# Routing of a mixture-of-experts block: the tokens' low parts formed by VectorE from PSUM instead of by GpSimd, and two selection chains interleaved

## The chip, the cores and the metric

The kernel is one program on one core of a Trainium2 chip. The core has a matrix engine (TensorE, PE in the rows; its weight loads are PEld), VectorE (DVE), ScalarE (ACT), GpSimd (POOL) and a queue that issues transfers (SP). Matrix products land in PSUM, which has eight banks per partition; all else is in SBUF. Each engine works through its own list of instructions in the order in which it was written or scheduled, and engines wait for each other by semaphores. The metric is device microseconds of one execution; the time of a kernel is the median of its runs.

## The reference, cut to what matters

Two layers over 256 tokens of width 1024. Each layer adds a mix of a convolution and two attentions, then a mixture of 16 experts in four groups. The change is in the routing of the experts:

```python
def grouped_moe(h, w_router, b_router, w_gate, w_up, w_down):
    aff = sigmoid(h @ w_router)
    biased = aff + b_router
    grp = biased.reshape(B, L, 4, 4)
    grp_score = sum(top_k(grp, 2)[0], axis=-1)          # sum of the two best of a group
    best = argmax(grp_score)                             # one group for each token
    in_grp = (arange(16) // 4) == best[..., None]
    _, top_idx = top_k(where(in_grp, biased, -inf), 2)   # its two best experts
    w = take(aff, top_idx); w = w / sum(w)
    ...
    for e in range(16):
        a = silu(h @ w_gate[e]) * (h @ w_up[e])
        out = out + gates[..., e:e+1] * (a @ w_down[e])
```

So a token picks the group whose two best scores have the largest sum, and in it the two experts with the best scores; ties go to the lower index.

## The kernel before, in words

**Weights.** All weights come from HBM through one ring of 14 buffers of 1 MB (`pump`, L77), issued on SP's queue in a fixed order: of a layer first the projections of the mixers and the modulation (ada) parts, then eight pairs of experts, for each pair four tiles of gate and up weights and two of down weights. A buffer that TensorE has finished (`done`) is issued again for the next tile in the list.

**A layer.** The mixers end with the output projection (L645) and the residual (L396), which also feeds the router's logits (L388, L392). Then `moe` begins with `route`. The token tile is transposed back to token-major order into four PSUM banks (`xtp[h, t]`, L901 and L903: half h of the columns, tokens t). In layer 1 these four banks are not given back, as the experts' results are later added onto them (`accs`). In `route`, VectorE works out scores, groups and experts; TensorE meanwhile runs matmuls for the next modulation vectors (`fill(2)`, L274).

**The tokens in two parts.** The gather needs the normalised tokens as a sum of a rounded value `gH` and its remainder `gL`. Before, ScalarE scales each bank into a tile `xs` (L798) and rounds it into `gH` (L799), and GpSimd forms `gL = xs - gH` (L800), four pieces of 128x512 in each layer.

**Selection.** It is two chains on VectorE. The first finds the group (L755 to L772: `hi`, `lo`, `m1` to `m3`, `gs`, `gm`, `ing`), on 2 to 16 elements a partition. The second counts for each expert how many of its group beat it (L779 to L784: `eql`, `gtr`, `ct`), on 128 elements. `slb` (L787) joins them to a 0/1 table in bf16.

**Counts, one-hots, gather.** TensorE turns `slb` into positions within each expert's block (L803 to L807). VectorE makes keys from them (L811 to L828), then `prep1(0)` writes the one-hot table `D` of the first four experts' pairs (L910). `prep4` gathers the tokens (L935): for each of eight column blocks four matmuls, `gH` and `gL` of token tile 0, then of tile 1, added up in PSUM; two column blocks share a bank. ScalarE evicts the first and third bank (L939), VectorE the second and fourth (L941). Then the experts of pair 0 start (L957), with the weights' buffers that wait for that.

**Layer 1 alone.** The vector g2 is spread over all partitions by two matmul groups (L883) into two banks, which VectorE adds to a table (L1110) right after `D`.

TensorE's and VectorE's orders in `moe` are as the code writes them (`manual_schedule`); ScalarE and GpSimd are ordered by the tile scheduler.

Of the kernel before, what the change touches and what calls it, by code (L numbers as in the profile page):

```python
# [9 lines left out]
F32 = mybir.dt.float32  # L10
# [3 lines left out]
AF = mybir.ActivationFunctionType  # L14
OP = mybir.AluOpType
# [4 lines left out]
P = 128  # L20
# [32 lines left out]
def block_kernel(ctx: ExitStack, tc: tile.TileContext, x, c, w_ada, b_ada, g_mix, w_in, w_dw, b_dw, ln_conv_g,  # L53
# [673 lines left out]
    def route(wk, router, xtp, gH, gL, fill):  # L727
# [16 lines left out]
        for t in range(NT):  # L744
# [7 lines left out]
        b8 = bi.rearrange("p t (g e) -> p (t g) e", e=4)  # L752
        hi = tmp([P, 8, 2], "hi")
        lo = tmp([P, 8, 2], "lo")
        V.tensor_tensor(hi, b8[:, :, 0:4:2], b8[:, :, 1:4:2], OP.max)  # L755
        V.tensor_tensor(lo, b8[:, :, 0:4:2], b8[:, :, 1:4:2], OP.min)
        m1 = tmp([P, 8], "m1")
# [4 lines left out]
        V.tensor_tensor(m3, lo[:, :, 0], lo[:, :, 1], OP.max)  # L762
        V.tensor_tensor(m2, m2, m3, OP.max)
        gs = tmp([P, NT, 4], "gs")
        V.tensor_tensor(gs.rearrange("p t g -> p (t g)"), m1, m2, OP.add)
        gm = tmp([P, NT, 1], "gm")
        V.tensor_reduce(gm[:, :, 0], gs, AX.X, OP.max)
        V.tensor_tensor(gs, gs, gm.to_broadcast([P, NT, 4]), OP.is_equal)
# [4 lines left out]

        shp = [P, 8, 4, 4]
        mine = b8[:, :, :, None].to_broadcast(shp)
        other = b8[:, :, None, :].to_broadcast(shp)
        gtr, eql = (wk.tile([P, FE], F32, name=n, tag="eac")[:, 0:8 * 16].rearrange("p (g a b) -> p g a b", g=8, a=4)
                    for n in ("gtr", "eql"))
        V.tensor_tensor(eql, other, mine, OP.is_equal)  # L779
        V.tensor_tensor(gtr, other, mine, OP.is_gt)  # L780
        V.tensor_tensor(eql, eql, low4[:, None, :, :].to_broadcast(shp), OP.mult)
        V.tensor_tensor(gtr, gtr, eql, OP.add)
        ct = wk.tile([P, FE], F32, name="ct", tag="eth", bufs=1)[:, 0:32].rearrange("p (g e) -> p g e", e=4)
        V.tensor_reduce(ct, gtr, AX.X, OP.add)  # L784
# [7 lines left out]
        for h in range(2):  # L792
            for t in range(NT):
                hs = slice(h * 512, (h + 1) * 512)
                if t == 0:
                    xs2 = wk.tile([P, NT, 512], F32, name="xs", tag="Yh")
                xs = xs2[:, t, :]
                S.activation(xs, xtp[h, t], AF.Copy, scale=rst[:, t:t + 1])  # L798
                S.copy(gH[:, t, hs], xs)  # L799
                G.tensor_tensor(gL[:, t, hs], xs, gH[:, t, hs].bitcast(F32), OP.subtract)  # L800
# [508 lines left out]
```

## Time and profile before

| | before |
|---|---|
| median of 3 runs | 592.02 us (590.42 to 594.18) |
| profiled execution | 592.18 us, span 590.5 us from first to last instruction |
| TensorE busy | 548.6 us, 93% of the span |
| VectorE busy | 277.8 us, 47% |
| ScalarE busy | 157.6 us, 27% |
| GpSimd busy | 46.0 us, 8% |
| HBM read | 180.92 MB, 308 GB/s over the span |
| mean granted clock of TensorE | 0.976 of full |

The routing of layer 0 stands at about 162 to 181 us of the span, that of layer 1 at about 442 to 460 us. The profile cannot be read from the busy shares alone: an engine with a small share can hold up the one that is nearly always busy, and it does so only in the stretches where that one stands idle. So the rows to look for are idle times of TensorE and what ended them.

### The profile page before, as it was taken

To read this page: it belongs to the slowest core of one execution; us is meant where nothing else is said; L and a number is where in the kernel's file an instruction comes from. 1 tells how busy PE (TensorE), PEld (TensorE's weight loads), DVE (VectorE), ACT (ScalarE), POOL (GpSimd) and SP (SyncE) were. 2 spreads that over 40 slices of the span, in tenths; PEclk is the share of its full clock that TensorE was granted. 3 is DMA by queue.
4 is the path that set the end of the run, shared out by engine and by line. 5 is a ranking of instruction groups with operands and counts; after the bars stand their busy time and mean duration, and the time that the engine had idled before them with its cause. 6 is when DMAs were issued, how large, how long until landed. Compare 5 with 4: busy or idle time off the path is not lost. (4 is left out here: it accounts for less than half of the span.)

```text
span 590.5 us, 10358 instructions
## 1 busy us (share of the span) xinstructions
PE 548.6 (93%) x3881; PEld 336.7 (57%) x3881; DVE 277.8 (47%) x882; ACT 157.6 (27%) x368; POOL 46.0 (8%) x51
## 2 busy tenths in 40 slices
PE   2889999999979999999969999999997999999993
PEld 0378886677735444444337788668774554444331
DVE  1321999574264433332133099956427533333222
ACT  1331103346242111111134021344624211111114
POOL 1000004000030000000000000500003011111110
PEclk9979999999989999999979999999998999999997
DMA  8999989973499999999999997957349699999932
GB/s 320 383 302 380 401 316 394 398 268 116 140 335 363 363 363 354 359 348 359 391 352 372 384 383 308 347 196 246 122 143 332 199 360 361 359 363 361 356 112 75
DMA packets 126025, 182.82 MB, mean 310 GB/s; under 512 B 7920, under 2 KB 94216, under 8 KB 125960
## 3 DMA queue, kind: packets, MB, share of 16 engines
q1 hardware_dynamic: 125344, 180.80, 88.2%
q10 hardware_dynamic: 616, 1.19, 0.5%
q8 instruction: 36, 0.59, 0.4%
q14 instruction: 29, 0.24, 0.1%
HBM read 180.92 MB, written 1.05 MB: 308 GB/s over the span
## 5 line engine op out<-in xcount | busy, mean ns | idle before, releaser
L957 PE MATMUL bank<-w,XT 128*32 128x512 f32 (+1 forms) x1024 | 112.9, 592 | 0.0
L431 PE MATMUL bank<-w,hT 128*128 128x256 f32 (+1 forms) x448 | 102.9, 390 | 1.1 <-ACT hT L407 1.1
L431 PEld LDWEIGHTS bank<-w,hT 128*128 128x128 f32 x448 | 85.6, 193 | 16.9 <-ACT hT L407 2.1
L957 PEld LDWEIGHTS bank<-w,XT 128*32 128x32 f32 x1024 | 33.6, 110 | 75.1 <-issue 69.3
L995 PE MATMUL bank<-w,eaT 128*32 128x512 f32 (+1 forms) x512 | 58.2, 595 | 0.4
L645 PE MATMUL bank<-yT,w 128*128 128x256 f32 x256 | 57.5, 381 | 0.0
L274 PE MATMUL bank<-w,cB 128*32 128x512 f32 x384 | 50.8, 641 | 5.7 <-DMA w<-in_w_ada 3.5
L645 PEld LDWEIGHTS bank<-yT,w 128*128 128x128 f32 x256 | 48.0, 190 | 6.8 <-issue 0.7
L674 DVE SCALAR_TENSOR_TENSOR cvy<-cva,hw,cvy 128x256 f32<-128x256 f32 x108 | 49.7, 509 | 0.6
L945 DVE SCALAR_TENSOR_TENSOR eac<-eth,bank 128x256 f32<-128x256 f32 x16 | 6.7, 421 | 83.5 <-ACT eth L944 83.5
L935 PE MATMUL bank<-D,gH 128*128 128x256 f32 x128 | 33.1, 297 | 2.4 <-DVE eac L945 2.4
L995 PEld LDWEIGHTS bank<-w,eaT 128*32 128x32 f32 x512 | 15.2, 110 | 32.0 <-issue 28.9
L944 ACT ACTIVATE eth<-bank 128x256 f32<-128x256 f32 x16 | 6.1, 384 | 96.2 <-PE bank L957 96.2
L935 PE MATMUL bank<-D,gL 128*128 128x256 f32 x128 | 31.2, 282 | 0.0
L939 ACT ACTIVATE XT<-bank,sh,sc 128x256 f32<-128x256 f32 x36 | 18.2, 560 | 44.4 <-PE bank L935 44.4
L935 PEld LDWEIGHTS bank<-D,gH 128*128 128x128 f32 x128 | 24.7, 193 | 6.7 <-issue 4.7
L446 PE MATMUL bank<-hT,w 128*128 128x256 f32 x128 | 28.3, 379 | 0.0
L446 PEld LDWEIGHTS bank<-hT,w 128*128 128x128 f32 x128 | 24.2, 190 | 3.3
L274 PEld LDWEIGHTS bank<-w,cB 128*32 128x32 f32 x384 | 10.6, 112 | 26.7 <-issue 16.5
L983 POOL TENSOR_TENSOR Yl<-yf,Yh 128x512 fp32r<-128x512 f32 x14 | 18.0, 1283 | 95.1 <-ACT Yh L982 95.1
L522 ACT ACTIVATE pr<-pr,nm 128x128 f32<-128x128 f32 (+1 forms) x48 | 21.3, 444 | 14.1 <-DVE nm L519 14.1
L935 PEld LDWEIGHTS bank<-D,gL 128*128 128x128 f32 x128 | 24.7, 193 | 0.2 <-issue 0.2
(268 smaller groups left out, 662.9 us busy)
## 6 DMA issues: line engine op xcount, KB each, us to landing
w<-in_w_ada SPq DMA_DIRECT2D x48, 1024.0 KB, 11.6
w<-in_w_gate SPq DMA_DIRECT2D x128, 256.0 KB, 6.1
w<-in_w_up SPq DMA_DIRECT2D x128, 256.0 KB, 5.9
w<-in_w_down SPq DMA_DIRECT2D x64, 512.0 KB, 7.5
w<-in_w_in SPq DMA_DIRECT2D x16, 1024.0 KB, 13.0
w<-in_w_o SPq DMA_DIRECT2D x8, 1024.0 KB, 9.1
w<-in_w_in SPq DMA_DIRECT2D x4, 328.0 KB, 15.8
xin<-in_x ACTq DMA_DIRECT2D x1, 1024.0 KB, 9.4
```

The costliest lines, as they stand in the source:

```text
L274: T.matmul(self.pa[j:j + 32, :], cB[:, 2 * kq + kk, o:o + 32], W[:, kk, h * 512:(h + 1) * 512], start=(u == 0 and kq == 0), stop=(u + 1 == ...
L431: T.matmul(pts[t], hT[:, k, tt], W[:, kk, :], start=first, stop=last)
L446: T.matmul(pp[:, cc, :], W[:, kk, cs], hT[:, k, :], start=(k == 0 and cc == 0), stop=(k == KT - 1 and cc == 1))
L522: S.activation(pr[:, lo:hi], pr[:, lo:hi], AF.Exp, bias=nm[:, u:u + 1], scale=-1.0, accum_out=sums[:, u:u + 1])
L645: T.matmul(pos[n // 2][:, n % 2, :], W[:, n * P:(n + 1) * P], yT[:, k, :], start=(ki == 0 and n % 2 == 0), stop=(ki == KT - 1 and n % 2 == 1))
L674: tap = V.scalar_tensor_tensor(out=cy[:, cc, :], in0=src, scalar=w, in1=cy[:, cc, :], op0=OP.mult, op1=OP.add)
L935: T.matmul(pg[:, i, :], z[:, t, ks], D[:, t, :], start=(si == 0), stop=(si == 3))
L939: S.activation(XT[:, k, :], pg[:, i, :], AF.Identity, bias=sh2[:, k:k + 1], scale=a2[:, k:k + 1])
L945: V.scalar_tensor_tensor(out=ac, in0=th, scalar=1.0, in1=pgu[:, 0, :], op0=OP.add, op1=OP.mult)
L957: T.matmul(pf[b0:b0 + BLK, :], XT[:, k, o + b0:o + b0 + BLK], W[:, e, k % 2, :], start=(k == 0), stop=(k == KT - 1))
L983: (V if whole else G).tensor_tensor(Yl[:, sl], yf, Yh[:, sl].bitcast(F32), OP.subtract)
L995: T.matmul(pd[b0:b0 + BLK, :], aT[:, f, b0:b0 + BLK], W[:, e, f, :], start=(f == 0), stop=(f == 1))
```

## The change

In `route`, the `xs` tile, the second ScalarE pass and GpSimd's subtraction are gone. ScalarE scales and rounds each PSUM bank straight into `gH` (four instructions a layer instead of eight). A generator `low()` forms `gL = bank * rst - gH` on VectorE, reading the PSUM bank; `moe` runs it right after `prep1(0)`, so behind `D` and ahead of the g2 additions and the gather's evictions. The selection's two chains are written alternately. Nothing else is touched.

```diff
--- before.py
+++ after.py
@@ -750,38 +750,38 @@
         V.scalar_tensor_tensor(out=bi, in0=aff, scalar=0.5, in1=brt[:, None, :].to_broadcast([P, NT, NE]), op0=OP.mult,
                                op1=OP.add)
         b8 = bi.rearrange("p t (g e) -> p (t g) e", e=4)
+
+        shp = [P, 8, 4, 4]
+        mine = b8[:, :, :, None].to_broadcast(shp)
+        other = b8[:, :, None, :].to_broadcast(shp)
+        gtr, eql = (wk.tile([P, FE], F32, name=n, tag="eac")[:, 0:8 * 16].rearrange("p (g a b) -> p g a b", g=8, a=4)
+                    for n in ("gtr", "eql"))
+        ct = wk.tile([P, FE], F32, name="ct", tag="eth", bufs=1)[:, 0:32].rearrange("p (g e) -> p g e", e=4)
         hi = tmp([P, 8, 2], "hi")
         lo = tmp([P, 8, 2], "lo")
         V.tensor_tensor(hi, b8[:, :, 0:4:2], b8[:, :, 1:4:2], OP.max)
         V.tensor_tensor(lo, b8[:, :, 0:4:2], b8[:, :, 1:4:2], OP.min)
+        V.tensor_tensor(eql, other, mine, OP.is_equal)
         m1 = tmp([P, 8], "m1")
         m2 = tmp([P, 8], "m2")
         m3 = tmp([P, 8], "m3")
         V.tensor_tensor(m1, hi[:, :, 0], hi[:, :, 1], OP.max)
         V.tensor_tensor(m2, hi[:, :, 0], hi[:, :, 1], OP.min)
         V.tensor_tensor(m3, lo[:, :, 0], lo[:, :, 1], OP.max)
+        V.tensor_tensor(gtr, other, mine, OP.is_gt)
         V.tensor_tensor(m2, m2, m3, OP.max)
+        V.tensor_tensor(eql, eql, low4[:, None, :, :].to_broadcast(shp), OP.mult)
         gs = tmp([P, NT, 4], "gs")
         V.tensor_tensor(gs.rearrange("p t g -> p (t g)"), m1, m2, OP.add)
+        V.tensor_tensor(gtr, gtr, eql, OP.add)
         gm = tmp([P, NT, 1], "gm")
         V.tensor_reduce(gm[:, :, 0], gs, AX.X, OP.max)
+        V.tensor_reduce(ct, gtr, AX.X, OP.add)
         V.tensor_tensor(gs, gs, gm.to_broadcast([P, NT, 4]), OP.is_equal)
         V.tensor_tensor(gs, gs, desc4[:, None, :].to_broadcast([P, NT, 4]), OP.mult)
         V.tensor_reduce(gm[:, :, 0], gs, AX.X, OP.max)
         ing = tmp([P, NT, 4], "ing")
         V.tensor_tensor(ing, gs, gm.to_broadcast([P, NT, 4]), OP.is_equal)
-
-        shp = [P, 8, 4, 4]
-        mine = b8[:, :, :, None].to_broadcast(shp)
-        other = b8[:, :, None, :].to_broadcast(shp)
-        gtr, eql = (wk.tile([P, FE], F32, name=n, tag="eac")[:, 0:8 * 16].rearrange("p (g a b) -> p g a b", g=8, a=4)
-                    for n in ("gtr", "eql"))
-        V.tensor_tensor(eql, other, mine, OP.is_equal)
-        V.tensor_tensor(gtr, other, mine, OP.is_gt)
-        V.tensor_tensor(eql, eql, low4[:, None, :, :].to_broadcast(shp), OP.mult)
-        V.tensor_tensor(gtr, gtr, eql, OP.add)
-        ct = wk.tile([P, FE], F32, name="ct", tag="eth", bufs=1)[:, 0:32].rearrange("p (g e) -> p g e", e=4)
-        V.tensor_reduce(ct, gtr, AX.X, OP.add)
         ingb = ing.rearrange("p t g -> p (t g)")[:, :, None].to_broadcast([P, 8, 4])
         slb = wk.tile([P, NT, NE], BF16, name="slb", tag="slb", bufs=1)
         V.scalar_tensor_tensor(out=slb.rearrange("p t (g e) -> p (t g) e", e=4), in0=ct, scalar=1.5, in1=ingb,
@@ -791,13 +791,7 @@
         fill(2)
         for h in range(2):
             for t in range(NT):
-                hs = slice(h * 512, (h + 1) * 512)
-                if t == 0:
-                    xs2 = wk.tile([P, NT, 512], F32, name="xs", tag="Yh")
-                xs = xs2[:, t, :]
-                S.activation(xs, xtp[h, t], AF.Copy, scale=rst[:, t:t + 1])
-                S.copy(gH[:, t, hs], xs)
-                G.tensor_tensor(gL[:, t, hs], xs, gH[:, t, hs].bitcast(F32), OP.subtract)
+                S.activation(gH[:, t, h * 512:(h + 1) * 512], xtp[h, t], AF.Copy, scale=rst[:, t:t + 1])
         slf = sl.rearrange("p (t g) e -> p t (g e)", t=NT)
         pk = bank([P, NT + 1, NE])
         T.matmul(pk[:, 0, :], tri, slb[:, 0, :], start=True, stop=True)
@@ -827,6 +821,14 @@
         V.tensor_copy(ky[:, :, :, 1:3], rk2)
         V.tensor_scalar(ky[:, :, :, 3], rk2[:, :, :, 1], float(-BLK), None, OP.add)
 
+        def low():
+            for h in range(2):
+                for t in range(NT):
+                    hs = slice(h * 512, (h + 1) * 512)
+                    V.scalar_tensor_tensor(out=gL[:, t, hs], in0=xtp[h, t], scalar=rst[:, t:t + 1],
+                                           in1=gH[:, t, hs].bitcast(F32), op0=OP.mult, op1=OP.subtract)
+                    yield
+
         def gates():
             S.activation(lg, lg, AF.Exp, scale=-1.0)
             V.tensor_scalar(lg, lg, 1.0, None, OP.add)
@@ -863,7 +865,7 @@
             V.tensor_scalar(fl[:, 0:1], m1x, CAP + 0.5, None, OP.is_gt)
             return fl, nb
 
-        return ky, gates, flags, rk, fi
+        return ky, gates, flags, rk, fi, low()
 
     def moe(big, wk, l, router, nxt, nnorm):
         a2, sh2 = mod["sc2", l], mod["sh2", l]
@@ -903,7 +905,7 @@
                         T.transpose(pt[:, j * P:(j + 1) * P], xk, ident)
                 xtp[h, t] = pt
 
-        ky, gates, flags_, rk, fi = route(wk, router, xtp, gH, gL, fill)
+        ky, gates, flags_, rk, fi, low = route(wk, router, xtp, gH, gL, fill)
         kyf = ky.rearrange("p t q b -> p t (q b)")
 
         def onehot(key, D, nb, w):
@@ -1106,6 +1108,8 @@
             gather(d["XT"], d["D"], 2 * P, kps, act)
 
         prep1(0)
+        for _ in low:
+            pass
         for h, pb in enumerate(g2ps):
             V.tensor_tensor(g2b[:, h * 512:(h + 1) * 512], pb, g2b[:, h * 512:(h + 1) * 512], OP.add)
         prep4(0, range(4))
```

How the order moves at three places. The first is VectorE in layer 0, within the selection; `bi` are the biased scores, `hi`, `lo`, `m`, `gs`, `gm`, `ing` belong to the group's chain, `eql`, `gtr`, `ct` to the count's. Before:

```order
L765 TENSOR_TENSOR gs<-m_1356,m_1357 128x8 [waits DVE_49]
L767 TENSOR_REDUCE gm<-gs 128x2 [waits DVE_49]
L768 TENSOR_TENSOR gs<-gs,gm 128x8 [waits DVE_49]
L769 TENSOR_TENSOR gs<-gs,desc_81 128x8 [waits DVE_49]
L770 TENSOR_REDUCE gm<-gs 128x2 [waits DVE_49]
L772 TENSOR_TENSOR ing<-gs,gm 128x8 [waits DVE_49]
L779 TENSOR_TENSOR eql<-bi 128x128
L780 TENSOR_TENSOR gtr<-bi 128x128
L781 TENSOR_TENSOR eql<-eql,low_82 128x128 [waits DVE_49]
L782 TENSOR_TENSOR gtr<-gtr,eql 128x128 [waits DVE_49]
L784 TENSOR_REDUCE ct<-gtr 128x32 [waits DVE_49]
L787 SCALAR_TENSOR_TENSOR slb<-ct,ing 128x32 [waits DVE_49]
```

and with the change:

```order
L764 TENSOR_TENSOR eql<-bi 128x128
L768 TENSOR_TENSOR m_1360<-hi 128x8 [waits DVE_49]
L769 TENSOR_TENSOR m_1361<-hi 128x8
L770 TENSOR_TENSOR m_1362<-lo 128x8 [waits DVE_49]
L771 TENSOR_TENSOR gtr<-bi 128x128
L772 TENSOR_TENSOR m_1361<-m_1361,m_1362 128x8 [waits DVE_49]
L773 TENSOR_TENSOR eql<-eql,low_82 128x128
L775 TENSOR_TENSOR gs<-m_1360,m_1361 128x8 [waits DVE_49]
L776 TENSOR_TENSOR gtr<-gtr,eql 128x128 [waits DVE_49]
L778 TENSOR_REDUCE gm<-gs 128x2 [waits DVE_49]
L779 TENSOR_REDUCE ct<-gtr 128x32 [waits DVE_49]
L780 TENSOR_TENSOR gs<-gs,gm 128x8 [waits DVE_49]
```

The five wide instructions stood in a row behind `ing`; now each stands between two small ones of the other chain.

The second is VectorE in layer 1, behind the keys `ky`; `bank_7844` and the three like it hold the transposed tokens, `rst` the tokens' scales. Before:

```order
L828 TENSOR_SCALAR ky<-rk 128x16
L910 TENSOR_TENSOR D<-iota_s,ky 128x512 [waits DVE_49]
L1110 TENSOR_TENSOR g2b<-bank_7969,g2b 128x512 [waits DMAHW3_49,PE_49]
L1110 TENSOR_TENSOR g2b<-bank_7971,g2b 128x512 [waits PE_49]
L941 TENSOR_SCALAR XT<-bank_8000,sc_1_7478,sh_1_7476 128x256 [waits PE_49]
```

and with the change:

```order
L912 TENSOR_TENSOR D<-iota_s,ky 128x512 [waits DVE_49]
L828 SCALAR_TENSOR_TENSOR gL<-bank_7844,rst,gH 128x512 [waits Activation_49]
L828 SCALAR_TENSOR_TENSOR gL<-bank_7856,rst,gH 128x512 [waits Activation_49]
L828 SCALAR_TENSOR_TENSOR gL<-bank_7861,rst,gH 128x512 [waits Activation_49]
L828 SCALAR_TENSOR_TENSOR gL<-bank_7866,rst,gH 128x512 [waits Activation_49]
L1114 TENSOR_TENSOR g2b<-bank_7953,g2b 128x512 [waits DMAHW3_49,PE_49]
L1114 TENSOR_TENSOR g2b<-bank_7955,g2b 128x512 [waits PE_49]
L943 TENSOR_SCALAR XT<-bank_7988,sc_1_7472,sh_1_7470 128x256 [waits PE_49]
```

Four instructions of 128x512 stand now between `D` and the g2 additions.

The third is TensorE in layer 1, the first gather; each bank takes eight matmuls, and the rows without a wait between those shown are cut. Before:

```order
L935 MATMUL bank_7989<-D,gH 128x256 [waits DVE_49,PE_49]
L935 MATMUL bank_7989<-D,gL 128x256 [waits Pool_49]
L935 MATMUL bank_7989<-D,gH 128x256
L935 MATMUL bank_7989<-D,gL 128x256 [waits Pool_49]
...
L935 MATMUL bank_8000<-D,gH 128x256 [waits DVE_49]
...
L935 MATMUL bank_8011<-D,gH 128x256 [waits DVE_49]
L935 MATMUL bank_8011<-D,gL 128x256 [waits Pool_49]
L935 MATMUL bank_8011<-D,gH 128x256 [waits Activation_49]
L935 MATMUL bank_8011<-D,gL 128x256 [waits Pool_49]
...
L935 MATMUL bank_8022<-D,gH 128x256 [waits Activation_49]
```

and with the change:

```order
L937 MATMUL bank_7977<-D,gH 128x256 [waits DVE_49,PE_49]
L937 MATMUL bank_7977<-D,gL 128x256 [waits DVE_49]
L937 MATMUL bank_7977<-D,gH 128x256
L937 MATMUL bank_7977<-D,gL 128x256 [waits DVE_49]
...
L937 MATMUL bank_7988<-D,gH 128x256 [waits Activation_49]
...
L937 MATMUL bank_7999<-D,gH 128x256 [waits DVE_49]
...
L937 MATMUL bank_8010<-D,gH 128x256 [waits DVE_49]
```

The `gL` matmuls of the first bank waited for GpSimd and now wait for VectorE. The second bank's first matmul waited for VectorE (the g2 addition that empties the bank it takes over); now it waits for ScalarE, because the built program puts it into the same PSUM bank as the first, which ScalarE empties. The third and fourth bank take over the two g2 banks.

## Rows read from the trace of the kernel before

**Rows 1.** The page's part 1: engine busy us (share of the span) xinstructions.

```profile
PE 548.6 (93%) x3881; PEld 336.7 (57%) x3881; DVE 277.8 (47%) x882; ACT 157.6 (27%) x368; POOL 46.0 (8%) x51
```

**Rows 2.** Timeline, layer 0 selection: start us, us, engine, line, op, out<-in, form, xcount.

```profile
166.94 5.18 POOL L800 TENSOR_TENSOR gL<-xs,gH 128x512 fp32r<-128x512 f32 x4 [69.88 <-DVE gs L769]
...
167.17 1.08 DVE L772 TENSOR_TENSOR ing<-gs,gm 128x8 f32<-128x8 f32 x1
...
168.17 0.28 DVE L779 TENSOR_TENSOR eql<-bi 128x128 f32<-128x128 f32 x1
168.37 1.36 DVE L780 TENSOR_TENSOR gtr<-bi 128x128 f32<-128x128 f32 x1
...
169.65 1.34 DVE L781 TENSOR_TENSOR eql<-eql,low 128x128 f32<-128x128 f32 x1
...
171.03 1.24 DVE L782 TENSOR_TENSOR gtr<-gtr,eql 128x128 f32<-128x128 f32 x1
...
172.87 0.17 PE L803 MATMUL bank<-slb,tri 128*128 128x16 bf16 x1 [3.96 <-DVE slb L787]
```

**Rows 3.** Timeline, layer 0: the first VectorE instructions on the scores.

```profile
165.41 0.18 DVE L755 TENSOR_TENSOR hi<-bi 128x16 f32<-128x16 f32 x1
165.50 0.17 DVE L756 TENSOR_TENSOR lo<-bi 128x16 f32<-128x16 f32 x1
...
165.62 0.17 DVE L760 TENSOR_TENSOR m<-hi 128x8 f32<-128x8 f32 x1
```

**Rows 4.** Timeline, layer 0: from the counts to the end of the first gather.

```profile
173.06 3.20 PE L274 MATMUL bank<-w,cB 128*32 128x512 f32 x16
...
174.66 0.69 DVE L910 TENSOR_TENSOR D<-iota_s,ky 128x512 fp32r<-128x512 f32 x1
...
176.79 0.37 PE L935 MATMUL bank<-D,gH 128*128 128x256 f32 x1
...
177.00 0.28 PE L935 MATMUL bank<-D,gL 128*128 128x256 f32 x1
...
180.29 0.28 PE L935 MATMUL bank<-D,gL 128*128 128x256 f32 x1
```

**Rows 5.** Timeline, layer 1: the same stage.

```profile
445.29 0.17 DVE L755 TENSOR_TENSOR hi<-bi 128x16 f32<-128x16 f32 x1
...
452.74 0.17 PE L803 MATMUL bank<-slb,tri 128*128 128x16 bf16 x1 [4.26 <-DVE slb L787]
...
452.87 3.20 PE L883 MATMUL bank<-adaev,selu 128*128 128x512 f32 x4
...
454.55 0.69 DVE L910 TENSOR_TENSOR D<-iota_s,ky 128x512 fp32r<-128x512 f32 x1
455.16 0.68 DVE L1110 TENSOR_TENSOR g2b<-bank,g2b 128x512 f32<-128x512 f32 x1
...
457.46 1.02 ACT L939 ACTIVATE XT<-bank,sh,sc 128x256 f32<-128x256 f32 x2 [7.45 <-PE bank L935]
...
459.97 0.28 PE L935 MATMUL bank<-D,gL 128*128 128x256 f32 x1
```

**Rows 6.** Line L986: instructions, duration ns min/median/max, first and last start us.

```profile
L986 DVE SCALAR_TENSOR_TENSOR Yl<-bank,gate,Yh x16: 750/750/752, 195.2 to 297.1; 128x512 fp32r<-128x512 f32 x16
```

**Rows 7.** Line L77 from 281.7 to 282.2 us: issue and landing.

```profile
L77 SPq DMA_DIRECT2D w<-in_w_down x1: 368/368/368, 281.6 to 281.6; - x1
...
DMA to landing us min/median/max: 9.1/9.1/9.1
```

**Rows 8.** Timeline of TensorE, 292 to 300 us: last pair's down projection, layer 0.

```profile
292.68 3.64 PE L995 MATMUL bank<-w,eaT 128*32 x32
```

**Rows 9.** Windows: us, busy us of each engine (xcount), PEclk, DMA share, GB/s.

```profile
174.00:176.00 2.00, 2.00 (x12) 0.21 (x4) 1.25 (x6) 0.00 (x0) 0.00 (x0) 0.50 1.11 369
```

**Rows 10.** Windows as before, 458 to 462 us in layer 1.

```profile
460.00:462.00 2.00, 2.00 (x23) 0.67 (x25) 1.63 (x5) 0.37 (x1) 0.00 (x0) 1.00 0.00 0
```

**Rows 11.** The page's part 5: the gather's weight loads.

```profile
L935 PEld LDWEIGHTS bank<-D,gL 128*128 128x128 f32 x128 | 24.7, 193 | 0.2 <-issue 0.2
```

## The prediction, made before the changed kernel was run

> **What bounds the kernel now.** I read the page first: TensorE is busy for 93% of the span, no other engine for half of it [rows 1]. A change on VectorE, ScalarE or GpSimd therefore counts only where TensorE waits. So I then read the list of what TensorE waited for: in the layer-0 stretch that begins with the routing no transfer stands in it, and the longest entry is `slb`, the selection's result. In both layers the first count matmul stands idle for it, 3.96 us and 4.26 us [rows 2, 5]. Third, the timeline of VectorE in that stretch tells why `slb` is late. `ing` on 128x8 takes 1.08 us, where its like on 128x8 takes 0.17 [rows 2, 3]; of the wide instructions one takes 0.28 us and the three behind it 1.36, 1.34 and 1.24, in the same form or nearly so. That lasts just as long as GpSimd's four subtractions, 166.94 to 172.12, and the one quick wide instruction begins where the first of those four has ended (about 1.3 us each, 5.18 in all). So VectorE is held up while GpSimd reads and writes: (1.08-0.17)+(1.36-0.28)+(1.34-0.28)+(1.24-0.28) = 4.0 us, the whole of TensorE's wait.
>
> **Part 1, GpSimd's subtractions go.** `slb` then comes as soon as its chain allows. The chain is 18 instructions from `hi` to `slb`, 13 small and 5 wide. If each waited for the one before (0.21 from `hi` to the `m` that needs it [rows 3]; 0.32 for a wide one, its 0.28 and the same hand-over), it would take 4.3 us. The ten that need each other give at least 2.1. Instructions that don't wait start 0.09 us after one another (`hi`, `lo` [rows 3]), wide ones 0.20 (`eql`, `gtr` [rows 2]); stepping the new order through with these gives 2.8 us, which I take, since the rows show the overlap. `slb` is there at 165.41+2.8 = 168.2 in layer 0 and 445.29+2.8 = 448.1 in layer 1. TensorE's fill matmuls end at 172.87-3.96 = 168.91 and 452.74-4.26 = 448.48, both later: the counts start there, and what the interleaving itself brings (some tenths) is hidden by the fill.
>
> A rule speaks against the interleaving: the Trainium skill ("VectorE: DVE Perf Modes", The DRAIN you can't avoid) says that the next VectorE instruction does not start until the pipe of the last has emptied, and advises fewer instructions. `lo` here starts while `hi` is running, so the trace does not bear it out for small independent ones; by the rule the sum below would be 2.0 us smaller.
>
> **Part 2, the low parts go on VectorE, behind `D`.** Counts, keys and `D` keep their lengths. `D` ended at 174.66+0.69 = 175.35 and at 455.24; 3.96 and 4.26 earlier that is 171.39 and 450.98. The trace has no `low`, but one with the same operands (128x512, PSUM bank, a scalar, a second tensor in SBUF): 0.75 us [rows 6]. From below the g2 addition bounds it, 0.68 [rows 5], from above 0.75 and the 1.06 that a held-up instruction lost. I take 0.75. The next starts about 0.08 us before the last has ended (`D` and the g2 addition [rows 5]), so 0.67 each. TensorE needs the first for its second matmul and the second for its fourth: D + 1.34, and an estimated 0.25 for the hand-over and the weight load of 0.19 [rows 11]. ScalarE does four instructions instead of eight on the same banks; the old series ended before `slb`, so the shorter one hides as well, and `gH` is never the late one.
>
> *Layer 0.* The fill of 16 matmuls took 3.20 us at half clock [rows 4, 9]; without the idle time before it I take full clock, so about 1.7, and it ends before `D`. The fourth gather matmul starts at 171.39+1.34+0.25 = 172.98. The other 28 start (180.29-177.00)/28 = 0.1175 us apart [rows 4], the last at 176.27 instead of 180.29: **4.0 us**. It is more than 3.96 less the 1.3 us of the lows because the old gather stood behind a slow fill and began at half clock.
>
> *Layer 1.* The fourth matmul starts at 450.98+1.59 = 452.57, the first bank's eighth at 453.04. The second bank may start only when ScalarE has emptied the first, as both take the same PSUM bank: 0.28 for the last matmul, 1.02 for two evictions [rows 5], 0.06 for the hand-over, so 454.40. Then 24 matmuls, the last at 457.09 instead of 459.97: **2.9 us**. The g2 additions wait behind the lows: these end at 450.98+2.68 = 453.66, the additions at 454.9, and the third bank, which needs the first of them, comes at 454.40+8x0.1175 = 455.3. So they cost nothing by 0.4 us or more; the g2 matmuls (3.20 us mostly at half clock) also end ahead of the lows. VectorE's evictions of the second and fourth bank come after that, and nothing behind them moves against the gather.
>
> **Does the gain arrive?** From the gather on TensorE works without a gap through the expert pairs, so a shift in layer 0 goes on, until a weight is late. The nearest case is the last down weight of layer 0: issued at 281.6, landed 9.1 later at 290.7 [rows 7]; its matmuls are the second half of a series of 3.64 us from 292.68, so from 294.5 [rows 8]. The queue is full there, so it won't land earlier: only 3.8 of the 4.0 us pass. In layer 1 transfers stand still at 460 to 462 us [rows 10], as all 14 buffers are full, until pair 0 frees the first; they resume as much earlier as TensorE does. Sum: 3.8+2.9 = 6.7 us off the profiled execution's 592.18 (span 590.5), which stands 0.16 above the median of the runs, 592.02. **Forecast: 585.5 us.** A measurement of this kernel can tell about 1% from no change, so 586.1 and 597.9 are the lines.
>
> **Rivals.**
> *The clock falls in the new, short gaps* (chance 0.22). TensorE still stands idle several times between the fill and the second bank. The granted clock fell to half after the 4 us of idling before, and matmuls were then 0.21 us apart instead of 0.1175 [rows 4, 9]. If half of the 24 in layer 1 run so, it costs 1.1 us: 586.6; with half of the 28 in layer 0, 587.9. Against it: the new gaps are 0.5 to 1.4 us, with matmuls between them. The Trainium skill ("TensorE: Matmul & The Clock Gate", A second HAM failure mode: psum-queue depth-cycling) speaks for it: short idle times between groups of matmuls while banks are cycled made the clock swing between its levels in another kernel.
> *Transfers take layer 0's gain* (0.10): TensorE starts the pairs earlier and meets weights that are not there. Then only layer 1's 2.9 us stay: 589.3. For it: the queues run at 369 GB/s [rows 9] all through layer 0. Against it: the 3.8 us of slack at the tightest tile.
> *VectorE is not held up by GpSimd* (0.04), but by something that stays; then `slb` is as late as before and the lows suffer the same. In layer 0 `D` ends at 175.35, two lows at 1.73 apart and 0.25 put the fourth matmul at 179.06 and the last at 182.35, 2.1 later than before; in layer 1 the same steps give 463.5, 3.5 later: 597.8, slower than before. It decides if the wide instructions stay above 1 us. Against it stands the quick `eql` between two subtractions.
> *VectorE overlaps nothing* (0.04): the chain takes 4.3 us, `slb` comes at 169.7 and 449.6, and 2.0 us of the gain go: 587.5. That is the rule above as a mechanism; `lo` beginning 0.09 us after `hi` speaks against it.
>
> **How the numbers follow.** My forecast has the other 0.60. Range 583.0 to 589.5: from below lows of 0.68 us, the full 4.0 and the runs' own scatter, from above the clock, the overlap and the transfers; out of it lie the slower rival and some of the tails. Faster by over 1%: two in three of my forecast (585.5 is only 0.6 below the line, and runs scatter more), a third of the clock's: 0.47. Slower by over 1%: half of the slower rival and a little more: 0.03. Within 1%: 0.50.
>
> **What the new profile would show.** GpSimd has no row in the routing. `ing` takes 0.17, the wide instructions 0.28 each; `slb` no longer stands in TensorE's waits, or with tenths. Four `gL` rows of about 0.75 us follow `D`. In layer 1 the gather breaks off after eight matmuls for about 1.3 us, released by ScalarE's `XT`, in layer 0 it doesn't. PEclk holds at 1.00 through both routings. The last gather matmul of layer 0 stands at 176.3, pair 0 of layer 1 starts 6.7 us earlier. I am wrong if wide instructions stay long, if TensorE waits for weights in the last pairs of layer 0, or if half clock shows in the gather.

## The result, and the profile after

The changed kernel takes 584.84 us (median of 5 runs, 584.41 to 585.19), the kernel before, beside it on the same chip, 592.02 (5 runs, 590.42 to 594.18): a ratio of 0.988, 95% interval [0.986, 0.989], 7.2 us. The forecast was 585.5, in a range of 583.0 to 589.5. In a later batch the changed kernel was timed again: 585.12 against 591.94, ratio 0.989 [0.987, 0.991].

The profiled execution has a span of 582.8 us, before it was 590.5. The page's part 1 answers [rows 1]; GpSimd has lost 10 us, TensorE 3:

```profile
PE 545.5 (94%) x3881; PEld 333.9 (57%) x3881; DVE 273.7 (47%) x890; ACT 153.6 (26%) x360; POOL 36.0 (6%) x43
```

VectorE, with eight more instructions of 128x512, is busy 4 us less. Its busy time before included waiting: the record of a held-up instruction contains its wait. The timeline of layer 0 shows it (columns as in [rows 2]), and answers [rows 2 to 4]:

```profile
164.77 0.17 DVE L762 TENSOR_TENSOR hi<-bi 128x16 f32<-128x16 f32 x1
164.87 0.17 DVE L763 TENSOR_TENSOR lo<-bi 128x16 f32<-128x16 f32 x1
...
165.38 0.28 DVE L771 TENSOR_TENSOR gtr<-bi 128x128 f32<-128x128 f32 x1
...
167.10 0.17 DVE L784 TENSOR_TENSOR ing<-gs,gm 128x8 f32<-128x8 f32 x1
...
167.31 0.19 DVE L787 SCALAR_TENSOR_TENSOR slb<-ct,ing 128x32 bf16<-128x32 f32 x1
...
168.20 0.18 PE L797 MATMUL bank<-slb,tri 128*128 128x16 bf16 x1
...
168.42 1.93 PE L274 MATMUL bank<-w,cB 128*32 128x512 f32 x16
...
170.03 0.69 DVE L912 TENSOR_TENSOR D<-iota_s,ky 128x512 fp32r<-128x512 f32 x1
...
170.64 2.72 DVE L828 SCALAR_TENSOR_TENSOR gL<-bank,rst,gH 128x512 fp32r<-128x512 f32 x4
...
170.87 0.36 PE L937 MATMUL bank<-D,gH 128*128 128x256 f32 x1 [0.53 <-DVE D L912]
171.44 0.39 PE L937 MATMUL bank<-D,gL 128*128 128x256 f32 x1 [0.21 <-DVE gL L828]
...
175.50 0.28 PE L937 MATMUL bank<-D,gL 128*128 128x256 f32 x1
```

`slb` is ready 167.50-164.77 = 2.73 us after `hi`, and the first count matmul (L797) no longer has a bracket, so it waits for nothing: the fill ran until then, 0.7 us longer than the selection. The four low parts take 2.72 us behind `D`: 0.74 each, and (2.72-0.74)/3 = 0.66 from one to the next. The executions begin the routing at slightly different times (`hi` at 165.41 before, 164.77 here), so a stage is measured from its `hi`: the last gather matmul comes 10.73 us after it, before 14.88 [rows 3, 4]. That is 4.15 us.

The same stage in layer 1, which answers [rows 5]:

```profile
441.62 0.18 DVE L762 TENSOR_TENSOR hi<-bi 128x16 f32<-128x16 f32 x1
...
444.75 0.18 PE L797 MATMUL bank<-slb,tri 128*128 128x16 bf16 x1
...
446.58 0.69 DVE L912 TENSOR_TENSOR D<-iota_s,ky 128x512 fp32r<-128x512 f32 x1
...
447.19 2.72 DVE L828 SCALAR_TENSOR_TENSOR gL<-bank,rst,gH 128x512 fp32r<-128x512 f32 x4
...
449.54 1.02 ACT L941 ACTIVATE XT<-bank,sh,sc 128x256 f32<-128x256 f32 x2 [4.06 <-PE bank L937]
...
450.61 0.39 PE L937 MATMUL bank<-D,gH 128*128 128x256 f32 x1 [1.11 <-ACT XT L941]
...
453.43 0.28 PE L937 MATMUL bank<-D,gL 128*128 128x256 f32 x1
```

Here the last gather matmul comes 11.81 us after `hi`, before 14.68: 2.87 us. The new wait of 1.11 us on ScalarE's `XT` is the one that layer 1 pays and layer 0 doesn't.

The windows give the clock (columns as in [rows 9]): the changed kernel's two routings, from `hi` to the first pair.

```profile
164.77:176.50 11.73, 10.84 (x97) 6.27 (x89) 8.99 (x37) 4.79 (x10) 0.00 (x0) 1.00 0.97 311
441.62:453.64 12.02, 10.04 (x70) 5.87 (x69) 9.50 (x37) 4.61 (x10) 0.00 (x0) 1.00 1.00 348
```

The granted clock is 1.00, 2.4 GHz, throughout. In the same two stretches of the kernel before it averaged 0.89:

```profile
165.41:181.29 15.88, 11.92 (x98) 6.67 (x88) 10.82 (x33) 6.86 (x14) 5.18 (x4) 0.89 1.00 340
445.29:460.18 14.89, 10.63 (x71) 6.53 (x69) 11.43 (x33) 6.58 (x14) 5.17 (x4) 0.89 0.83 286
```

**The whole difference** of the two profiled spans, 7.69 us: start up to the first `hi` 0.64, routing of layer 0 up to the first pair 4.15 (15.88 to 11.73), of layer 1 2.87 (14.89 to 12.02), the end of the program behind the last overflow branch 1.30 (13.45 to 12.15); lost are 0.81 at layer 0's overflow branch (from the last down projection's last matmul to the first combine matmul: 4.27 to 5.08), and together 0.5 in the pairs, the second mixer and the last branch. The start varies by up to 1.1 us between two executions of the same kernel, and the branch of the changed one by 0.7, as the table behind the experiments shows.

### The profile page after: what moved, and what is told of

It reads as the page before. It is cut to its first block, busy times and chain, and to the rows that moved or that the text cites. A ratio compares the mean times of both kernels' runs of the same rounds, so it can differ in the third digit from the quotient of the medians.

```text
span 582.8 us, 10343 instructions
## 1 busy us (share of the span) xinstructions
PE 545.5 (94%) x3881; PEld 333.9 (57%) x3881; DVE 273.7 (47%) x890; ACT 153.6 (26%) x360; POOL 36.0 (6%) x43
## 6 DMA issues: line engine op xcount, KB each, us to landing
w<-in_w_ada SPq DMA_DIRECT2D x48, 1024.0 KB, 11.6
```

## The experiments

My theory: before the change GpSimd's subtractions, by reading SBUF, held up VectorE's selection; that, and not the place of the work as such, was the loss. Rivals: the order of the two chains was what mattered; the gather had waited for GpSimd's result; any work on GpSimd does harm. The first four kernels tell these apart.

**Low parts alone (e1).** The low parts as in the change, the selection's chains one after the other (against the changed kernel, shortened; the remarks stand for the lines left out):

```diff
-        V.tensor_tensor(eql, other, mine, OP.is_equal)   # between lo and m1; likewise gtr, eql, gtr, ct
...
         V.tensor_tensor(ing, gs, gm.to_broadcast([P, NT, 4]), OP.is_equal)
+        V.tensor_tensor(eql, other, mine, OP.is_equal)   # then gtr, eql, gtr, ct
```

> The low parts are formed on VectorE from PSUM as in the change, but the two chains of the selection stand one after the other, as before. Theory: GpSimd holding up VectorE was the whole matter. Without it the serial selection should take about 3.5 us from hi to slb (2.73 in the changed kernel); TensorE's fill ends 3.5 us (layer 0) and 3.2 us (layer 1) after hi, so TensorE waits only 0.2 to 0.5 us more per layer: 585 to 586 us. Rival: the interleaving brings about half of the gain: 588 to 589 us. In both, every wide operation takes 0.28 to 0.29 us.

Measured: 585.27 us against 592.33, ratio 0.990 [0.988, 0.993]. `slb` is ready 3.41 us after `hi` (2.73 in the changed kernel), about the 3.5 that I expected. In layer 0 `D` comes 5.27 us after `hi`, in the changed kernel 5.26: nothing is lost, the fill hides it all. In layer 1 the list of TensorE's waits (first columns: what waited, for what; then us in total, times, longest) has a new entry:

```profile
PE bank L797 <- DVE slb L787: 0.3, 1, 0.3
```

So the interleaving is worth 0.68 us on VectorE, of which 0.3 reach TensorE, in one layer. The time can't be told from that of the change: the gain is that of the moved low parts, and the rival that the interleaving brings half of it is out.

**Interleaving alone (e2).** The changed order of the selection, with `xs`, its copy and GpSimd's subtraction as before.

> The two chains of the selection are issued in turn, the subtraction stays on GpSimd. Theory: the wide operations now run ahead of GpSimd's first subtraction (which starts 1.5 us after hi), but four of the small operations with two operands in SBUF are then held up by one subtraction of 1.28 us each, so slb is ready some 6.5 us after hi and the gather has its low parts no earlier: 591 to 592 us, no gain that counts. Rival: the order was what mattered, the selection ends 2.7 us after hi and the gather starts with the second subtraction: 587 to 589 us.

Measured: 590.74 us, ratio 0.998 [0.996, 1.000]: little, about as expected. The theory's mechanism is in VectorE's timeline of layer 0, the tail of the selection:

```profile
167.74 1.10 DVE L780 TENSOR_TENSOR gs<-gs,gm 128x8 f32<-128x8 f32 x1
168.87 1.20 DVE L781 TENSOR_TENSOR gs<-gs,desc 128x8 f32<-128x8 f32 x1
170.11 0.16 DVE L782 TENSOR_REDUCE gm<-gs 128x2 f32<-128x8 f32 x1
170.31 0.99 DVE L784 TENSOR_TENSOR ing<-gs,gm 128x8 f32<-128x8 f32 x1
171.33 1.21 DVE L787 SCALAR_TENSOR_TENSOR slb<-ct,ing 128x32 bf16<-128x32 f32 x1
```

The four wide instructions with two inputs are through before GpSimd starts at 167.53; now four small ones, of 128x8 and 128x32, take 1.0 to 1.2 us, one for each subtraction. `slb` is ready 172.54-166.00 = 6.54 us after `hi` (7.40 before), as expected, and TensorE waits 3.1 us for it. In layer 0 the first pair starts no earlier than before (16.12 us after `hi`, before 15.88). Behind this wait the fill (3.57 us up to the gather) and the first nine gather matmuls ran at half clock; before, of the gather only the first three did:

```profile
172.81:176.38 3.57, 3.57 (x19) 0.59 (x16) 1.98 (x10) 0.00 (x0) 0.00 (x0) 0.50 1.09 361
176.38:178.47 2.09, 2.09 (x13) 2.09 (x10) 0.00 (x0) 0.59 (x1) 0.00 (x0) 0.50 1.08 366
```

In layer 1 the first pair starts 1.7 us earlier.

**Useless reads on GpSimd (e3)**, in the changed kernel behind each of ScalarE's high parts; nothing uses `xs2`:

```diff
+                G.tensor_tensor(xs2[:, t, :], gH[:, t, hs].bitcast(F32), gH[:, t, hs].bitcast(F32), OP.subtract)
```

> The changed kernel with four useless GpSimd subtractions of 128x512, both operands in SBUF, behind ScalarE's four high parts, so that GpSimd works during the selection again while no result of it is needed. Theory: GpSimd's reading of SBUF holds up VectorE. Four operations with two operands in SBUF wait for one subtraction each (about 1.3 us), slb is ready 7 to 8 us after hi in place of 2.73, TensorE waits some 4.5 us behind the fill in each layer: 592 to 595 us, at least as slow as before the change. Rival: what cost time before was that the gather waited for GpSimd's result; then nothing waits here: 584.5 to 586 us, wide operations 0.28 us.

Measured: 592.31 us, ratio 1.000 [0.998, 1.002]. The whole gain is gone, though no result of GpSimd is waited for. VectorE and GpSimd in layer 0:

```profile
166.03 4.45 POOL L798 TENSOR_TENSOR xs<-gH 128x512 f32<-128x512 f32 x4 [68.80 <-ACT gH L794]
...
166.12 1.01 DVE L770 TENSOR_TENSOR m<-lo 128x8 f32<-128x8 f32 x1
167.06 0.28 DVE L771 TENSOR_TENSOR gtr<-bi 128x128 f32<-128x128 f32 x1
167.26 1.00 DVE L772 TENSOR_TENSOR m<-m,m 128x8 f32<-128x8 f32 x1
168.18 0.28 DVE L773 TENSOR_TENSOR eql<-eql,low 128x128 f32<-128x128 f32 x1
```

Each subtraction (1.08 to 1.16 us long) stretches one VectorE instruction, and one to three others run at their usual length before the next is stretched. `slb` is ready 5.74 us after `hi` and not 7 to 8: these subtractions are shorter than the 1.3 us that I took, and in part they run beside instructions that they don't hold up. TensorE's waits:

```profile
PE bank L801 <- DVE slb L787: 2.3, 1, 2.3
PE bank L801 <- DVE slb L787: 2.6, 1, 2.6
```

The first is layer 0, the second layer 1; I had expected 4.5 in each. The rest of the 7.5 us is no wait for `slb`. In layer 1 the granted clock was still 0.98 between 455.5 and 457.0; then, behind further waits of 0.6 us for `D` and 1.1 for `XT`, 14 gather matmuls ran at half of it,

```profile
457.04:460.19 3.15, 3.15 (x14) 3.15 (x15) 1.48 (x3) 0.00 (x0) 0.00 (x0) 0.50 0.30 101
```

which cost 3.15-14x0.1175 = 1.5 us; about 1.2 more lie at the end of the program. (The profiled execution, 593.62 us, is 1.3 above the median; its second mixer is 1.6 us longer than that of the changed kernel, and no run here shows why.) That the time fell into the range I gave (592 to 595) is thus partly luck: the waits were about half as long as I took them to be, and these two terms, which I hadn't counted, filled the gap.

**Useless writes on GpSimd (e4)**: three `G.memset(xs2[:, t, :], 0.0)` in each of the same four places.

> The changed kernel with twelve useless GpSimd memsets of 128x512 in the same place (estimate 0.45 us each, from 0.42 us for 128x384 at the start of the program, 5.4 us together, as long as the four subtractions). Theory: only what GpSimd reads from SBUF holds VectorE up, so nothing changes: 584.5 to 586 us, slb 2.7 to 2.9 us after hi. Rival: any work on GpSimd holds it up, reading or writing: 592 to 595 us. The Trainium skill (SBUF - State Buffer, on the shared port pair) says that a VectorE operation with two SBUF inputs contends only with a GpSimd operation that reads SBUF; by it this run equals the changed kernel.

Measured: 584.15 us, ratio 0.986 [0.984, 0.989], the changed kernel's time. `slb` is ready 2.71 us after `hi`. The twelve memsets did not wait for ScalarE and began earlier than I meant, but they ran until 162.44+5.65 = 168.09, over all of the wide instructions:

```profile
162.44 5.65 POOL L798 MEMSET xs<- 128x512 f32 x12 [64.94 <-PE bank L392]
...
167.05 0.29 DVE L776 TENSOR_TENSOR gtr<-gtr,eql 128x128 f32<-128x128 f32 x1
```

So it isn't work on GpSimd as such that held these instructions up. A memset differs from a subtraction in more than the reading, but the reading is what the theory names, and no run here speaks against it. The Trainium skill ("SBUF — State Buffer", SBUF: two separate sides) has the rule: a VectorE instruction with two SBUF inputs contends with a GpSimd instruction only if that one reads SBUF. e3 and e4 agree with it: `m` takes 1.01 us in e3 and 0.15 in e4.

**The subtraction later (e11).** Chains in turn, GpSimd subtracts as before, but begins only when `slb` is there:

```diff
+                G.tensor_copy(gL[:, t, hs.start:hs.start + 1], slb[:, 0, 0:1])
                 G.tensor_tensor(gL[:, t, hs], xs, gH[:, t, hs].bitcast(F32), OP.subtract)
```

> Chains in turn, and the subtraction stays on GpSimd but begins only when the selection is ready (a one-column copy of slb ahead of each subtraction). Theory: GpSimd's reading holds up VectorE wherever it falls: now the operations with two SBUF operands on the way to the one-hot (dl twice, ky, D) wait for one subtraction each, D starts 7 to 8 us after hi (5.26 in the changed kernel) and the last gather matmul comes some 12.4 us after it in both layers: 586.5 to 589 us. Rival: only the selection was the matter; D starts 5.3 us after hi, the gather follows the subtractions: 585 to 586 us.

Measured: 592.08 us, ratio 1.000 [0.998, 1.002], worse than I expected; the profiled execution, 589.74 us, is the fastest of ten. The selection is as quick as in the changed kernel (`slb` ready 2.72 us after `hi`), and the time is lost right behind it, on the keys:

```profile
167.74 4.95 POOL L801 TENSOR_TENSOR gL<-xs,gH 128x512 fp32r<-128x512 f32 x4
...
168.32 0.73 DVE L814 CAST fi<-f 1x8 int32<-1x8 f32 x1
...
169.17 1.12 DVE L822 TENSOR_SCALAR a<-rk 128x16 f32<-128x16 f32 x1
...
170.32 1.19 DVE L824 SCALAR_TENSOR_TENSOR dl<-rk,a 128x16 f32<-128x16 f32 x1
...
171.54 1.18 DVE L826 TENSOR_TENSOR dl<-dl,f 128x16 f32<-128x16 f32 x1
...
173.15 0.69 DVE L911 TENSOR_TENSOR D<-iota_s,ky 128x512 fp32r<-128x512 f32 x1
...
173.98 0.55 PE L936 MATMUL bank<-D,gH 128*128 128x256 f32 x1 [4.05 <-DVE D L911]
```

Again four subtractions hold up four instructions, and `D` begins 8.78 us after `hi` (5.26 in the changed kernel, 7 to 8 expected). Behind the wait of 4.05 us in layer 0 the gather also ran at half clock up to 178.81, which I hadn't counted: 4.83-22x0.1175 = 2.2 us. So its last matmul comes 15.59 us after `hi`, in layer 1, at full clock, 13.33 (12.4 expected in both):

```profile
173.98:178.81 4.83, 4.83 (x22) 4.83 (x23) 1.00 (x2) 1.02 (x2) 0.00 (x0) 0.50 1.07 377
```

Over the selection's wide instructions (before), over its tail (e2) and over the keys (e11) the subtractions cost most of the gain or all of it. Other places on GpSimd, behind `D` for one, were not tried.

**What is left in the changed kernel (e5 to e9).** e5 is the changed kernel itself, beside the next three.

> The changed kernel once more, beside the next three on the same chip. Theory: 584 to 586 us. It shows besides which differences between the profiled executions are its own: the start up to the first routing, the wait at the overflow branch (4.2 to 5.1 us in the runs so far) and the end of the program (11.6 to 13.5 us behind the last branch).

585.12 us, 0.989 [0.987, 0.991]. The distances from `hi` are the same to 0.01 us; what varies is in the table below.

e6 takes away the two waits that the change brought, on the low parts and on the shared bank (shortened):

```diff
+        lows = low()
+        next(lows)                       # behind the counts' matmuls, ahead of f
...
-        for _ in low:
-            pass
+        next(low)
         for h, pb in enumerate(g2ps):
             V.tensor_tensor(g2b[:, h * 512:(h + 1) * 512], pb, g2b[:, h * 512:(h + 1) * 512], OP.add)
+        for _ in low:
+            pass
```

> The changed kernel, with the first low part issued ahead of the counts (VectorE waits 0.93 and 0.63 us for them there), and in layer 1 the two g2b additions between the first two low parts and the last two, so that the gather's second bank is another than the first. Theory: the layer-1 gather waits for ScalarE only because its first two tiles share a bank; without that 1.11 us, and with the waits for low parts (0.22 and 0.16 us) gone, the last gather matmul comes 10.1 to 10.4 us after hi in layer 1 (11.81 now) and 10.3 to 10.5 in layer 0 (10.73 now): 1.7 to 2.0 us faster than the changed kernel, 582.8 to 583.3 us. Rival: the wait only moves to the later low parts, which the additions hold up by 1.28 us: no gain.

583.38 us, 0.986 [0.984, 0.988]. The last gather matmul comes 10.06 us after `hi` in layer 0 and 10.39 in layer 1: 0.67 and 1.42 less, together 2.1. In layer 1:

```profile
448.80 1.28 DVE L1116 TENSOR_TENSOR g2b<-bank,g2b 128x512 f32<-128x512 f32 x2
449.84 1.02 ACT L943 ACTIVATE XT<-bank,sh,sc 128x256 f32<-128x256 f32 x2 [3.41 <-PE bank L939]
450.00 1.40 DVE L806 SCALAR_TENSOR_TENSOR gL<-bank,rst,gH 128x512 fp32r<-128x512 f32 x2
...
451.45 0.38 PE L939 MATMUL bank<-D,gL 128*128 128x256 f32 x1 [0.16 <-DVE gL L806]
```

The second bank no longer waits for `XT`, and of the rival only 0.16 us is seen. But a new entry stands in the waits of layer 0's last pairs, and it is larger in e8:

```profile
PE bank L961 <- DMA w<-in_w_up: 0.2, 1, 0.2
PE bank L959 <- DMA w<-in_w_up: 1.1, 1, 1.1
```

e7 moves one step of the fill, eight matmuls, behind the counts; e8 has this and the g2 additions between the second and third low part:

```diff
-                nxt.take(TAKE[i - 2])
+                nxt.take(((4, 3), (2, 1))[last][i - 2])
```

> The changed kernel, with one step of TensorE's fill (eight matmuls, 0.96 us) moved from ahead of the counts to behind them in each layer. Theory: the selection is now ready 0.7 us (layer 0) and 0.4 us (layer 1) before the counts start, because the fill is longer than the selection; with the shorter fill D comes that much earlier, the last gather matmul comes 0.7 us earlier in layer 0 and 0.4 in layer 1: about 583.7 us. If the fill was no longer too long, it makes no difference: 584.8 us.

> The shorter fill together with the g2b additions between the low parts, all four low parts behind D. Theory: both gains add: 1.1 us from the fill and about 1.0 us more in layer 1, where the last gather matmul comes 10.3 to 10.5 us after hi (11.81 in the changed kernel): 582.6 to 582.9 us. Rival: the later low parts take the place of the bank as the wait: 583.7 us, as with the shorter fill alone.

e7: 583.82 us, 0.987 [0.984, 0.989]; the last gather matmul at 9.93 us in layer 0 (0.8 less) and 11.59 in layer 1 (0.2 less instead of 0.4: the g2 matmuls need ScalarE's copy of the shifted step, and the gather stands behind them). e8: 584.18 us, 0.986 [0.984, 0.989]; 10.06 and 10.68. Its two gains of 0.7 and 1.1 don't show as such in the time (584.18 against e5's 585.12); 1.1 of them go into the wait for `w_up` above. By their times alone e6, e7 and e8 can't be told from the changed kernel.

e9 joins what was good: e6, and the shorter fill in layer 0 only.

> The first low part ahead of the counts and the g2b additions between the low parts, as in the run with these two, and in layer 0 alone the fill shorter by one step (in layer 1 the shorter fill made the gather later). Theory: in layer 0 the last gather matmul comes 9.7 to 9.9 us after hi (10.06 without the shorter fill), in layer 1 10.4 us; but w_up's last transfers are nearly late by now (0.2 us of waiting in that run, 1.1 us in the one with the fill and g2b), so that most of these 0.3 us come back as a wait for the transfers: 583.0 to 583.4 us. Rival: the transfers are no limit, and 0.3 us is gained in full, 582.9 us; or they bind harder with each step that the routing gets shorter, 583.5 to 584.5 us.

583.14 us, 0.983 [0.980, 0.985]; 9.71 us after `hi` in layer 0, 10.40 in layer 1, and in this execution TensorE waits for no expert's weight. Its interval, beside the kernel before in a later batch, lies below that of e5, the changed kernel; from e6 the time doesn't tell it apart. By its time it is the version to keep.

**The kernel before again (e10)**, for its profile.

> The kernel before, once more, for its profile. Theory: what differs between the two profiles outside of the routing (the wait at the overflow branch, 4.27 us before and 5.08 after, and the end behind the last branch, 13.45 and 12.15 us) is a matter of the single execution: the branch again between 4.2 and 5.1 us, the end between 11.6 and 13.5 us, gather and first expert at the same distance from hi as in the first profile within 0.5 us. Rival: the end is 13.4 us in every profile of this kernel, so that a part of the gain lies there.

592.44 us against 592.35. The distances from `hi` hold within 0.03 us, but for the end the rival was right: 13.54 us, as in the first profile. From the traces, in us (start: up to the first `hi`; branch: last down projection's last matmul of layer 0 to the first combine matmul; mixer: from there to layer 1's `hi`; end: first combine matmul behind the last branch to the end of the span):

| kernel | start | hi to pair 0, layer 0 | layer 1 | branch | mixer | end |
|---|---|---|---|---|---|---|
| before | 165.41 | 15.88 | 14.89 | 4.27 | 145.28 | 13.45 |
| before again (e10) | 164.29 | 15.85 | 14.88 | 4.26 | 145.46 | 13.54 |
| interleaving alone (e2) | 166.00 | 16.12 | 13.17 | 4.18 | 145.73 | 13.34 |
| useless reads (e3) | 165.59 | 14.07 | 16.13 | 4.24 | 147.06 | 13.34 |
| later subtraction (e11) | 164.37 | 16.58 | 13.54 | 4.32 | 144.42 | 13.34 |
| changed | 164.77 | 11.73 | 12.02 | 5.08 | 145.50 | 12.15 |
| changed again (e5) | 165.28 | 11.73 | 12.01 | 4.39 | 145.65 | 12.15 |
| low parts alone (e1) | 164.83 | 11.73 | 12.33 | 4.23 | 146.06 | 12.71 |
| useless writes (e4) | 165.84 | 11.72 | 12.01 | 4.83 | 145.92 | 11.61 |
| e6 | 165.90 | 11.06 | 10.60 | 4.53 | 146.18 | 11.59 |
| e7 | 164.89 | 10.93 | 11.80 | 4.53 | 146.00 | 12.32 |
| e8 | 165.69 | 11.06 | 10.89 | 4.42 | 146.01 | 11.75 |
| e9 | 165.85 | 10.71 | 10.60 | 5.19 | 145.51 | 12.70 |

The start differs by up to 1.7 us between executions. The mixer agrees within 0.2 us in the two pairs of executions of one kernel, but differs by up to 2.6 us between kernels; no run here shows why. Both are as large as what e6 to e9 gain, so a single span says little about those.

The end is 13.3 to 13.5 us in all five executions of kernels with GpSimd's reads, and 11.6 to 12.7 in the eight without. The clock differs, here in the eight combine matmuls behind the branch of the kernel before and of the change:

```profile
577.01:583.17 6.16, 4.29 (x8) 1.79 (x8) 1.45 (x3) 3.67 (x9) 0.00 (x0) 0.72 0.02 5
570.62:575.50 4.88, 3.16 (x8) 1.32 (x8) 1.35 (x3) 3.42 (x8) 0.00 (x0) 1.00 0.03 7
```

TensorE had stood idle at the branch, and the clock falls soon after, ahead of the last three matmuls (0.85 us apart in the kernel before, 0.43 to 0.53 in the change) or only behind them. It fell ahead of them in the five with GpSimd's reads, and also in e1 and e9. Besides, TensorE pauses once more among these eight matmuls, for 0.9 to 2.0 us: in the five after the fourth, in the other eight after the fifth. Nothing here shows what decides either; it stays open, and is 0.6 to 2.0 us.

## Why the prediction was right

The mechanism of the routing held step by step, and the size to 0.7 us (584.84 for 585.5). It came out 1.2% faster; for more than 1% I had given 0.47. That the total fits so well is in part luck: small errors within the two layers and larger terms outside of the routing cancel, as the list shows.

- **VectorE was held up by GpSimd:** confirmed by the change (wide instructions 0.28 and 0.29, `ing` 0.17), and by e3 against e4. The rival that something else held it up is out.
- **`slb` 2.8 us after `hi`:** 2.73. Independent instructions overlap (`lo` begins 0.10 us behind `hi`, which takes 0.17), and even the serial selection of e1 took no more than 3.22+0.19 = 3.41 us. The rival in which each waits for the one before, 4.3, is out. The rule that the prediction set beside it was only half told: the Trainium skill ("VectorE: DVE Perf Modes", The DRAIN you can't avoid) adds that a next instruction which is not held starts earlier. With that the trace agrees; when the pipe is empty the rows don't show.
- **The interleaving is hidden by the fill:** in layer 0 wholly; in layer 1 it would be missed by 0.3 us (e1).
- **Low parts of 0.75 us, 0.67 apart:** 0.74 and 0.66.
- **Layer 0, 4.0 us:** 4.15 measured. The gather's first matmul waits for `D` (0.53), the second for the first low part (0.21). The estimated 0.25 for the hand-over and the weight load was too much: the fourth matmul starts 172.10-170.72 = 1.38 us behind the end of `D`, not 1.59. The fill takes 1.93 at full clock, I took 1.7.
- **Layer 1, 2.9 us:** 2.87. The second bank starts 8.99 us after `hi`, predicted 9.11, and waits for ScalarE; the 24 matmuls from there take 0.1 us more than priced, so the two cancel. The g2 additions cost nothing there.
- **0.2 us lost to the last down weight:** not lost. I had said that it wouldn't land earlier. Its issue came 2.0 us earlier in the span, at 279.6 (0.6 of that is the earlier start), and it landed 9.9 later, at 289.5 and not 290.7 [rows 7]:

```profile
L77 SPq DMA_DIRECT2D w<-in_w_down x1: 368/368/368, 279.6 to 279.6; - x1
...
DMA to landing us min/median/max: 9.9/9.9/9.9
```

  Its matmuls start at about 289.8, so 0.3 us are left of the 3.8. The rival that transfers eat layer 0's gain didn't come here, but it wasn't wrong in kind: where e6 and e8 go on, TensorE waits for `w_up`, 0.2 and 1.1 us.
- **The clock rival (0.22) didn't come:** waits of 0.2 to 1.1 us left the clock up in both routings. Its price was about right: e3, whose waits in layer 1 are 2.6, 0.6 and 1.1 us, paid 1.5.
- **Not in my sum:** the end of the program, 1.3 us shorter, and the branch, 0.1 to 0.8 us longer. In the profiled pair they nearly cancel with the 0.5 us of the pairs, the mixer and the last branch, and nothing in the forecast foresaw that; the 0.5 us between 6.7 and the 7.2 of the medians is of the size of layer 0's 4.15 for 3.8 and of what the end varies by. I treated everything behind layer 1's gather as unmoved, while the end ran at either clock.

## What to carry to other kernels

When a short instruction suddenly takes a microsecond, suspect that it is held up: look for the instruction on another engine that ends when it ends, and ask of that one whether it reads SBUF. Work on GpSimd that read SBUF was not free here while VectorE had a chain from SBUF on the critical path, at none of the places tried; a version on VectorE that takes one operand from PSUM (0.66 us apart here) beat the one handed over to GpSimd (1.3 us each, and about 1 us of VectorE's time besides). When a stage gets shorter, go through the next things in line at once, here a shared PSUM bank, a fill that is now too long, and weights that arrive just in time.

## What the runs showed of the hardware

- The size of the instruction that is held up hardly matters: on 128x8 it took 1.0 to 1.2 us instead of 0.17 (e2, e3; the last in e3 0.68), and in e11 `fi`, eight numbers on one partition, 0.73 and 1.01 instead of 0.16. In each of these stretches, and in the kernel before, four subtractions held up four VectorE instructions; between two that were held up, none to three ran at their usual length.
- It isn't only instructions with two SBUF inputs. In e11 `a`, one of 128x16 with a constant, took 1.12 us (0.17 in the changed kernel), and `fi` is a copy with one input. `f`, with a constant like `a` but read from PSUM, took its usual 0.17 beside the first subtraction, and reductions with one input from SBUF were not held up either: 0.16 for `gm` in e2 and 0.29 for `ct` in e3, beside running subtractions. No run here shows what sets the reductions apart. The Trainium skill ("SBUF — State Buffer", SBUF: two separate sides) names, beside two SBUF inputs, VectorE's two-port modes as a ground for contention; the traces don't show an instruction's mode.
- GpSimd's subtraction of `xs` and `gH` took 1.27 to 1.29 us in e2 and e11 (the shortest 1.26) and 1.29 to 1.40 before; the one of e3, which reads `gH` twice, 1.08 to 1.16. No run here shows what sets these lengths.
